# Low parts of the projection weights: kept in HBM by the first unit of tokens and read back by the second, in place of a second subtraction

## The chip, the cores and the metric

The kernel runs on one core of a Trainium2 chip. The metric is the device time of one execution in microseconds (us), the median of the runs shown. A core has a matrix engine (TensorE, PE in the profile; PEld is its weight load), three engines for elementwise work (VectorE or DVE, ScalarE or ACT, GpSimd or POOL), and SyncE (SP), which here issues every DMA, one after the other in the order in which they were emitted. An instruction that has to wait holds up what stands behind it on its engine.

## What is computed

The reference is a trunk of two layers over 2048 tokens of 1024 channels, all in float32. Cut to what matters:

```python
for i in range(2):
    h = rmsnorm(x, norm_g[i]) * (1.0 + scale) + shift        # scale, shift, gate from c
    out = rglru_block(h, ...) if i == 0 else gated_deltanet_block(h, ...)
    x = x + gate * out
return rmsnorm(x, final_g)

# both blocks begin with a projection:  proj = h @ in_w
#   layer 0: in_w is 1024 x 2048, then a causal convolution over 4 tokens, gates, a linear recurrence
#   layer 1: in_w is 1024 x 4096 (q, k, v, z) and 16 columns more, then the convolution and a
#            recurrence over chunks with a 128 x 128 state for each of 8 heads
```

## The kernel before, in words

**Splitting into high and low parts.** A float32 product is made of three matmuls on a faster, shorter type (float32r): each operand is split into a high part (the value rounded to that type) and a low part (the value minus its high part), and high times high, high times low and low times high are added up in PSUM; low times low is left out. `products` (line 646) emits these three matmuls for each of the 8 blocks of 128 input channels, 24 matmuls of 128 x 512 for one panel and one half of the tokens.

**Panels and units.** The weights of a projection are cut into panels of 128 output channels, 128 partitions x 1024 values, 512 KB. The tokens are cut into two units of 1024, and each unit into two halves of 512. The order of the whole program is: projection of layer 0 for unit 0 (`in1, 0`: 16 panels, called x and z) and for unit 1 (`in1, 1`), its output projection, projection of layer 1 for unit 0 (`in2, 0`: 32 panels, called k, v, q and z) and for unit 1 (`in2, 1`), and the last output projection. So each of the 48 panels is used twice, once in each unit, far apart in time.

**Getting a panel ready.** `panels_thread` (line 614) does this for every panel of every unit: SP loads it into a buffer `raw` (line 610), ACT rounds it into `whi` (line 639), and POOL subtracts, `wlo = raw - whi` (line 642). `raw`, `whi` and `wlo` have two buffers each. A new panel is begun when the panel two before it has made its last product; the third panel and the first and last two of a unit are loaded somewhat ahead. A panel makes two jobs of 24 matmuls, one for each half of the tokens.

**The other work of the stages.** In layer 0 each product of an x panel goes through ACT (copy to `xe`), POOL (first tap of the convolution, line 727), three more taps on DVE (line 701), then a split of its own (ACT `xh`, line 751; DVE `xl`, line 754) before the matmuls of the gates (`pg`, line 760). Besides, DVE sums rows of the conditioning weights (`acc`, line 415), which end in small matmuls (`adapt`, line 283). In layer 1 the same taps (line 701) make k, v and q; DVE inverts triangular blocks (`ttmp`, `tblk`, lines 1228 and 1231; a chain of small operations that each wait for the one before), and the recurrence passes between PE (`pp`, `py`, `pS`), DVE (`zt`, line 1357; `state`, line 1390) and ACT. Blocks are turned by way of HBM: `blk_d`, `tt_d`, `ac`, `v_d`, `q_d` are small transfers out and back on SP's queue.

**What sets the order.** The program is emitted by a planner (`Weave`, line 66). Every piece of work is a thread that yields the engine and an estimated duration before each step; the planner emits the step with the earliest estimated start. So the order on every engine is fixed when the program is built, from the estimates (2.3 us for the subtraction of a panel on POOL, for example). On the chip each engine runs its list in order and waits where data or a buffer is not there yet. The estimates know nothing of one engine slowing another.

Of the kernel before, what the change touches and what calls it, by code (L numbers as in the profile page):

```python
# [16 lines left out]
P = 128  # L17
# [24 lines left out]
class Slots:  # L42
    """The buffers of a tag, taken in turn."""
# [5 lines left out]
class Hold:  # L49
    """A buffer with several last readers."""  # L50
# [15 lines left out]
class Weave:  # L66
    """Emits threads of instructions in the order of their estimated start.

    Before each step a thread yields the engine, its duration and optionally the latency
    until the next step may start; for a transfer "sp", its bytes and whether to wait for  # L70
    its end. It yields an Event to wait for it, and Slots to take a buffer of them.
    """
# [66 lines left out]
def trunk_kernel(ctx, tc, x, c, ada_w, ada_b, ada_c, norm_c, final_g, w1, cw1, cb1, gate_w, gate_b, lam, ow1,  # L139
# [18 lines left out]
    def f(ap):  # L158
        return ap.bitcast(F32)
# [4 lines left out]
    # constants  # L164
# [37 lines left out]
    # tags: pool and number of buffers  # L202
# [11 lines left out]
    # free after the queries, before the recurrence ends  # L214
# [36 lines left out]
    def softplus(out, src, e, d):  # L251
        # max(x, 0) + log1p(exp(-|x|)), log1p(e) = 2 atanh(e / (2 + e))
        m = out
        dve.tensor_scalar(m, src, 0.0, None, ALU.min)
        dve.scalar_tensor_tensor(m, m, 2.0, src, ALU.mult, ALU.subtract)
        act.activation(e, m, AF.Exp)
        dve.tensor_scalar(d, e, 2.0, None, ALU.add)
        dve.reciprocal(out=d, in_=d)
        dve.tensor_tensor(e, e, d, ALU.mult)
        dve.tensor_tensor(d, e, e, ALU.mult)  # L260
        dve.tensor_scalar(m, d, 2.0 / 17.0, 2.0 / 15.0, ALU.mult, ALU.add)
        for q in (13, 11, 9, 7, 5, 3, 1):
            dve.tensor_tensor(m, m, d, ALU.mult)
            dve.tensor_scalar(m, m, 2.0 / q, None, ALU.add)
        dve.tensor_tensor(m, m, e, ALU.mult)
        dve.scalar_tensor_tensor(out, src, 0.0, m, ALU.max, ALU.add)

# [1 line left out]
    def finish_columns(layer, part, d, src):  # L269
        # bias, and for the scale (1 + scale) * norm_g  # L270
# [9 lines left out]
    def columns_of(acc, pt):  # L280
        # sums over the partitions, four columns of 128 channels
        for q in range(4):
            pe.matmul(pt[:, q:q + 1], lhsT=acc[:, q * P:(q + 1) * P], rhs=ones[:, 0:1], start=True, stop=True)
# [3 lines left out]
    def first_loads_thread():  # L287
        # scale and shift of the first layer, in the order in which they are needed
# [35 lines left out]
    def first_pe_thread():  # L324
        # scale, by the tensor engine
# [22 lines left out]
    def first_dve_thread():  # L348
        # shift, by DVE and the ones
# [47 lines left out]
    def row_halves_thread(parts):  # L397
        # halves of the other conditioning rows, summed over the channels of c by DVE and the ones
# [73 lines left out]
    def norm_thread(key, layer, src, t0, slot, before, after, xtags=("b4",) * TB, htag="hf"):  # L472
        # before: what the loads wait for; after: what the writes wait for
# [46 lines left out]
    def turned_thread(key, layer, src, t0, slot, before, between, after):  # L520
        # the norm of a tile, transposed ahead by 32 x 32 blocks, the blocks by way of memory
# [32 lines left out]
    def later(gen):  # L554
        # after the last transfer issued
        yield "none", w.free["dma"] + w.SEEN - w.now
        yield from gen
# [26 lines left out]
    # the panels of each unit in order, and its products: panel, half of the tokens  # L584
# [29 lines left out]
    def panels_thread():  # L614
        yield ev("adaissue", 2)
        ahead = []
        for name, panels, _ in plans:
            for m, p in enumerate(panels):
                # the third waits for the pair before it and is loaded ahead
# [15 lines left out]
                raw, rtok = ahead.pop(0)  # L635
                yield ev("raw", name, p)
# [3 lines left out]
                yield "pool", 2.3  # L640
                lo = tile_([P, KT, P], "wlo", "wlo", F32R)
                pool.tensor_tensor(lo, raw, f(hi), ALU.subtract)  # L642
                put("raw", rtok)
                w.set(ev("w", name, p), (hi, lo, htok, ltok))

    def products(pt, lhs, rhs, wait=None, dur=MM):
        # (hi + lo) * (hi + lo) without lo * lo
# [33 lines left out]
    def project_thread():  # L681
        for name, panels, jobs in plans:
# [3 lines left out]
            for n in range(len(jobs)):  # L686
                if name == ("in1", 0) and n < 2:
                    # the first two side by side, as the channels arrive
# [14 lines left out]
    def extend(xe, pt, mtok, carry, key, g):  # L703
        # the last columns of the half before, and the product
# [220 lines left out]
    def phase1_end_thread():  # L925
        # the memory of the first layer goes to the second
# [118 lines left out]
    def key_thread(u, h, i):  # L1045
        beta, gs, eg = yield ev("dec", u)
        # decay factors between the tokens of a chunk
# [19 lines left out]
        # row norms of k  # L1067
# [34 lines left out]
        # products of the keys  # L1102
# [22 lines left out]
        # k decayed to the end of the chunk  # L1125
# [30 lines left out]
    def tokens_of(ap, name):  # L1156
        # to token layout: transposed by 32 x 32 blocks, the blocks by way of memory
# [12 lines left out]
    def value_thread(u, h, i):  # L1170
        # v over the norm of k
# [33 lines left out]
    def inverses_thread(u, h):  # L1205
        # inverses of the 32 x 32 unit triangles on the diagonal
# [36 lines left out]
    def levels_thread(u, h):  # L1243
        # the transposed inverse takes the place of the transposed triangle, block by block
# [78 lines left out]
    def recurrence_thread(u, h):  # L1323
# [4 lines left out]
        for i in range(NTC):  # L1328
# [7 lines left out]
            for b in range(TB):  # L1336
                m = i * TB + b
                # no state before the first chunk, none needed after the last
# [21 lines left out]
                # a bank of PSUM is read by one engine at a time  # L1360
# [56 lines left out]
    def outputs_thread(u, h, i, oo, otok, so, sotok):  # L1417
# [14 lines left out]
        # transposed by 32 x 32 blocks: channel (e, i) of token (g, j) goes to partition (g, i)  # L1432
# [65 lines left out]
    def gated_thread(b, on, tok, zs, ztok):  # L1498
# [3 lines left out]
        # the blocks of the first units before the phase begins, in the place of panels  # L1502
# [26 lines left out]
    def out2_jobs():  # L1529
        nb = S // P  # L1530
        # the last columns in smaller parts
# [190 lines left out]
```

## Time and profile before

| | |
|---|---|
| time, median of 3 runs | 2044.7 us (2042.34 to 2049.82) |
| span of the profiled execution | 2033.7 us, 11.0 us under that median |
| busy in it | PE 1881.4 us (93%), DVE 1578.4 (78%), ACT 1019.8 (50%), POOL 945.0 (46%) |
| moved by DMA | 263.99 MB; read from HBM 186.38 MB, written 75.50 MB |
| subtraction of a panel on POOL | 96 times, 243.5 us in all |

The profile is of one execution. Its rows are read as follows. A group's row gives line, engine, operation, what it writes and reads, shape and count, then busy time and mean duration in ns, then how long the engine had been idle before these instructions and what ended that. A timeline row gives start, duration, engine, line, and in square brackets the engine's idle time before it and who ended it. A row of stretches gives the length, then busy time (and instructions) of PE, PEld, DVE, ACT and POOL, the granted clock of PE (1.00 is full speed), the busy share of the DMA engines and GB/s. The stages, as the panels' matmuls show them, are about: `in1, 0` from the start to 286 us, `in1, 1` to 536, the output projection to 725, `in2, 0` to 1276, `in2, 1` to 1838, and the last output projection.

### The profile page before, as it was taken

The page shows a single profiled execution, that of the slowest core. Times are in us where ns is not written, and L with a number is a line of the kernel's source. Part 1 is how long each engine was busy: PE and PEld are TensorE (multiplying, and loading weights), DVE is VectorE, ACT ScalarE, POOL GpSimd, SP SyncE. Part 2 cuts the span into 40 slices and gives each one's busy share as a digit, 9 for nine tenths or more (in the row PEclk, how much of TensorE's full clock was granted, in tenths as well). Part 3 has the DMA queues.
Part 4 walks back from the last instruction along what each step waited for, and adds up shares of the span by engine and source line. Part 5 has one row for each costly group of instructions (what it writes and reads, how often), then busy time and mean ns, then how long its engine had stood idle before and what let it go on. Part 6 is the DMA issues. An engine that isn't in the chain of part 4 may idle for free.

```text
span 2033.7 us, 31640 instructions
## 1 busy us (share of the span) xinstructions
PE 1881.4 (93%) x10408; PEld 1526.0 (75%) x10408; DVE 1578.4 (78%) x3176; ACT 1019.8 (50%) x2449; POOL 945.0 (46%) x1487
## 2 busy tenths in 40 slices
PE   6989889888999999999999999998999999999998
PEld 3777667676787777777787787777878777778887
DVE  6788998987744556988887988778888879887654
ACT  3656566454611224456565555554655555655311
POOL 4565665645400137545454653474455546531101
PEclk9999989989999999999999999999999999999999
DMA  8254524333368813436663436343334333466761
GB/s 315 60 150 128 186 98 134 122 109 119 125 195 215 252 54 96 102 70 148 143 144 82 89 86 173 84 113 93 69 91 104 90 79 83 111 184 210 227 197 63
DMA packets 493132, 263.99 MB, mean 130 GB/s; under 512 B 369188, under 2 KB 437028, under 8 KB 492968
## 3 DMA queue, kind: packets, MB, share of 16 engines
q1 hardware_dynamic: 492968, 261.97, 46.7%
q8 instruction: 82, 1.34, 0.3%
q14 instruction: 82, 0.67, 0.1%
HBM read 186.38 MB, written 75.50 MB: 129 GB/s over the span
## 4 chain that ended last, share of the span: by engine, by line
PE 39%; DVE 27%; DMA 8%; POOL 7%; issue 7%; ACT 6%; SPq 3%; DVEq 0%; POOLq 0%; ACTq 0%
PE mm L653 16%; PE mmo L653 12%; DVE xf L701 7%; DVE tblk L1231 3%; DVE ttmp L1228 3%; PE pg L760 2%; DMA raw<-in_w 2%; POOL wlo L642 1%; DVE ec L1100 1%; DMA xt_d<-xb 1%; SPq L515 1%; DVE acc L415 1%; POOL tz L798 1%; POOL xf L727 1%; DMA xt<-x_d 1%
## 5 line engine op out<-in xcount | busy, mean ns | idle before, releaser
L701 DVE SCALAR_TENSOR_TENSOR xf<-xe,cw_s,xf 128x512 f32<-128x512 f32 x384 | 359.8, 940 | 47.7 <-POOL xf L727 24.6
L642 POOL TENSOR_TENSOR wlo<-raw,whi 128x1024 fp32r<-128x1024 f32 x96 | 243.5, 2537 | 134.9 <-ACT whi L639 119.1
L1231 DVE TENSOR_TENSOR tblk<-tblk,ttmp 128x60 f32<-128x60 f32 (+24 forms) x496 | 144.3, 291 | 10.9 <-POOL tblk L1222 0.5
L1228 DVE TENSOR_TENSOR ttmp<-blk,tblk 128x60 f32<-128x60 f32 (+24 forms) x496 | 123.0, 248 | 16.9 <-DMA blk<-blk_d 6.5
L639 ACT CAST whi<-raw 128x1024 fp32r<-128x1024 f32 x96 | 100.2, 1044 | 47.3 <-DMA raw<-in_w 42.9
L716 POOL COPY carry<-xe 128x4 f32<-128x4 f32 x128 | 41.3, 322 | 170.6 <-ACT xe L713 158.8
L713 ACT COPY xe<-mm 128x512 f32<-128x512 f32 x128 | 74.1, 579 | 83.8 <-PE mm L653 79.8
L653 PE MATMUL mmo<-oh,yh 128*128 128x512 f32 x256 | 100.9, 394 | 5.1 <-DVE xr L908 4.7
L653 PE MATMUL mm<-hl_('in2', 1)_12407,whi 128*128 128x512 f32 x256 | 104.8, 410 | 0.0
L653 PE MATMUL mm<-hh_('in2', 0)_5394,whi 128*128 128x512 f32 x256 | 104.7, 409 | 0.0
L653 PE MATMUL mm<-hh_('in2', 0)_5171,whi 128*128 128x512 f32 x256 | 104.3, 407 | 0.3 <-ACT xe L713 0.3
L653 PE MATMUL mm<-hl_('in2', 0)_5395,whi 128*128 128x512 f32 x256 | 104.2, 407 | 0.0
L653 PE MATMUL mm<-hl_('in2', 1)_12235,whi 128*128 128x512 f32 x256 | 104.2, 407 | 0.0
L653 PE MATMUL mm<-hh_('in2', 0)_5394,wlo 128*128 128x512 f32 x256 | 104.1, 407 | 0.0
L653 PE MATMUL mm<-hh_('in2', 1)_12406,whi 128*128 128x512 f32 x256 | 104.0, 406 | 0.0
L653 PE MATMUL mm<-hl_('in2', 0)_5172,whi 128*128 128x512 f32 x256 | 103.8, 406 | 0.0
L653 PE MATMUL mm<-hh_('in2', 0)_5171,wlo 128*128 128x512 f32 x256 | 103.8, 405 | 0.0
L653 PE MATMUL mm<-hh_('in2', 1)_12234,whi 128*128 128x512 f32 x256 | 103.4, 404 | 0.2 <-DVE tz L972 0.2
L653 PE MATMUL mm<-hh_('in2', 1)_12406,wlo 128*128 128x512 f32 x256 | 103.6, 405 | 0.0
L653 PE MATMUL mm<-hh_('in2', 1)_12234,wlo 128*128 128x512 f32 x256 | 103.5, 404 | 0.0
L653 PE MATMUL mmo<-ol,oh 128*128 128x512 f32 (+1 forms) x264 | 102.1, 387 | 0.0
L653 PE MATMUL mmo<-oh,yl 128*128 128x512 f32 x256 | 100.8, 394 | 1.4 <-DVE yl L882 1.4
(326 smaller groups left out, 5910.8 us busy)
## 6 DMA issues: line engine op xcount, KB each, us to landing
raw<-in_w SPq DMA_DIRECT2D x96, 512.0 KB, 4.0
araw<-in_ada_w SPq DMA_DIRECT2D x32, 512.0 KB, 3.7
xt<-x_d SPq DMA_DIRECT2D x32, 512.0 KB, 4.5
xt_d<-xb SPq DMA_DIRECT2D x192, 64.0 KB, 2.4
xk<-xt_d SPq DMA_DIRECT2D x24, 512.0 KB, 4.7
xt<-in_x SPq DMA_DIRECT2D x16, 512.0 KB, 5.3
ada<-in_ada_w SPq DMA_DIRECT2D x16, 512.0 KB, 8.9
y_d<-tz SPq DMA_DIRECT2D x32, 256.0 KB, 2.7
```

The costliest lines, as they stand in the source:

```text
L415: dve.scalar_tensor_tensor(acc, raw[:, k, :], ck, acc, ALU.mult, ALU.add)
L515: sp.dma_start(out=dst[c_], in_=tb[32 * c_:32 * c_ + 32])
L639: act.copy(hi, raw)
L642: pool.tensor_tensor(lo, raw, f(hi), ALU.subtract)
L653: pe.matmul(pt, lhsT=lhs[a][:, k, :], rhs=rhs[b][:, k, :], start=(k == 0 and n == 0), stop=(k == KT - 1 and n == 2))
L701: dve.scalar_tensor_tensor(xf, xe[:, 1 + j:1 + j + TC], wc[:, j:j + 1], xf, ALU.mult, ALU.add)
L713: act.copy(xe[:, 4:4 + TC], pt)
L716: pool.tensor_copy(out=carry, in_=xe[:, TC:TC + 4])
L727: pool.tensor_scalar(xf, xe[:, 1:1 + TC], cw1_s[:, n, 0:1], cb1_s[:, n:n + 1], ALU.mult, ALU.add)
L760: pe.matmul(pg, lhsT=a[:, g, :], rhs=b, start=(q == 0), stop=(q == 2))
L1228: dve.tensor_tensor(tmp, blk[:, j, j + 1:32].unsqueeze(2).to_broadcast([P, r, c_]), t[:, j, 0:c_].unsqueeze(1).to_broadcast([P, r, c_]), A ...
L1231: dve.tensor_tensor(t[:, j + 1:32, 0:c_], t[:, j + 1:32, 0:c_], tmp, ALU.subtract)
```

## The change

In the first unit of tokens the low part is still made by the subtraction; after it, SP writes it to an HBM buffer of its own, one for each of the 48 panels (`keep_thread`). In the second unit there is no subtraction: SP reads that buffer into `wlo`, and the load of `raw` and the rounding into `whi` stay. The buffer `raw` is given back after the rounding in the second unit. In numbers of instructions: 48 subtractions of 128 x 1024 on POOL fewer, 48 DMA writes and 48 DMA reads of 512 KB more, all on SP's queue. The values of the low parts are the same. The diff, without lines of comment:

```diff
                 raw, rtok = ahead.pop(0)
+                lo = tile_([P, KT, P], "wlo", "wlo", F32R)
+                if name[1] > 0:
+                    kept = yield ev("kept", p)
+                    yield "sp", 512 * KB, False
+                    sp.dma_start(out=f(lo), in_=kept)
+                    w.spawn(arrive_thread(ev("lo", name, p)), 0)
                 yield ev("raw", name, p)
                 yield "act", 0.95
                 hi = tile_([P, KT, P], "whi", "whi", F32R)
                 act.copy(hi, raw)
-                yield "pool", 2.3
-                lo = tile_([P, KT, P], "wlo", "wlo", F32R)
-                pool.tensor_tensor(lo, raw, f(hi), ALU.subtract)
-                put("raw", rtok)
+                if name[1] > 0:
+                    put("raw", rtok)
+                    yield ev("lo", name, p)
+                else:
+                    yield "pool", 2.3
+                    pool.tensor_tensor(lo, raw, f(hi), ALU.subtract)
+                    put("raw", rtok)
+                    w.spawn(keep_thread(p, lo), 5)
                 w.set(ev("w", name, p), (hi, lo, htok, ltok))
 
+    def keep_thread(p, lo):
+        kept = dram.tile([P, KT, P], F32, name=f"wlo_d{p[0]}{p[1]}{p[2]}")
+        yield "sp", 512 * KB
+        sp.dma_start(out=kept, in_=f(lo))
+        w.set(ev("kept", p), kept)
```

Since the planner counts with other steps now, the order moves a little on every engine. Three places matter for what follows; in all rows a number behind `x` is how many such instructions stand in a row, and line numbers from 639 of the old file on stand 7 to 17 higher in the new one.

POOL in `in1, 1`, from the split of the gate weights (`gl`) of the last but one block of channels to that of the last, before:

```order
L828 TENSOR_TENSOR gl<-gw,gh 128x256
L798 TENSOR_TENSOR tz<-tz,tg 128x512
L716 COPY carry_109<-xe_3817 128x4
L727 TENSOR_SCALAR xf_3842<-xe_3817,cw_s,cb_s 128x512
L642 TENSOR_TENSOR wlo<-raw_3819,whi 128x1024
L778 TENSOR_SCALAR th<-th 128x512
L642 TENSOR_TENSOR wlo<-raw_3901,whi 128x1024
L828 TENSOR_TENSOR gl<-gw,gh 128x256
```

and the same stretch with the change:

```order
L845 TENSOR_TENSOR gl<-gw,gh 128x256
L815 TENSOR_TENSOR tz<-tz,tg 128x512
L728 COPY xe_3858<-carry_109 128x4
L733 COPY carry_109<-xe_3858 128x4
L744 TENSOR_SCALAR xf_3873<-xe_3858,cw_s,cb_s 128x512
L795 TENSOR_SCALAR th<-th 128x512 x2
L811 COPY hcar<-tg 128x1
L815 TENSOR_TENSOR tz<-tz,tg 128x512
L728 COPY xe_4025<-carry_109 128x4
L733 COPY carry_109<-xe_4025 128x4
L744 TENSOR_SCALAR xf_4044<-xe_4025,cw_s,cb_s 128x512
L845 TENSOR_TENSOR gl<-gw,gh 128x256
```

The two subtractions are gone, and the steps of the next block (`xe`, `carry`, `xf`) have moved up into their place.

SP in `in2, 1`, around the load of the panel q of head 4 (`tt_d` and `ac` are the way out and back of the inverted blocks, `blk_d` the way out of the next ones), before:

```order
L1239 DMA tt_d<-ttmp 256x1x32 x4
L1252 DMA ac<-tt_d 32x4x32 x3
L610 DMA raw_16082<-in_w 128x1024
L1252 DMA ac<-tt_d 32x4x32 x5
L1444 DMA o_d<-ob 32x16x32 x4
L1122 DMA blk_d<-ac 32x4x32 x3
```

and with the change:

```order
L1256 DMA tt_d<-ttmp 256x1x32 x4
L1461 DMA o_d<-ob 32x16x32 x3
L1269 DMA ac<-tt_d 32x4x32 x6
L610 DMA raw_16192<-in_w 128x1024
L641 DMA wlo<-wlo_d2q_9069 128x1024
L1269 DMA ac<-tt_d 32x4x32 x2
L1461 DMA o_d<-ob 32x16x32
L1139 DMA blk_d<-ac 32x4x32 x4
```

The read of the low part stands right behind the load of `raw`, and the last two `ac` and all of `blk_d` stand behind it.

SP in `in1, 0`, around the loads of the third and the fourth panel (`raw`), before:

```order
L820 DMA gw<-in_gate_w 128x256
L610 DMA raw_399<-in_w 128x1024
L530 DMA xt<-in_x 128x1024 x2
L610 DMA raw_674<-in_w 128x1024
L515 DMA xt_d<-xb 32x16x32 x8
```

and with the change:

```order
L837 DMA gw<-in_gate_w 128x256
L660 DMA wlo_d1x_356<-wlo 128x1024
L610 DMA raw_402<-in_w 128x1024
L660 DMA wlo_d1z_386<-wlo 128x1024
L530 DMA xt<-in_x 128x1024 x2
L660 DMA wlo_d1x_646<-wlo 128x1024
L610 DMA raw_680<-in_w 128x1024
L515 DMA xt_d<-xb 32x16x32 x8
```

The writes of the low parts of the first three panels stand between the loads now; the one of the third stands ahead of the second load.

## The prediction

> **What bounds the kernel now.** I read the page first, then the busy time by stage, then who PE waits for in the second unit's stages, then the rows around those waits. The page:
>
> ```profile
> span 2033.7 us, 31640 instructions
> PE 1881.4 (93%) x10408; PEld 1526.0 (75%) x10408; DVE 1578.4 (78%) x3176; ACT 1019.8 (50%) x2449; POOL 945.0 (46%) x1487
> ```
>
> PE is busy for 93% of the span, so nothing that leaves its work alone can gain more than its idle time and what it loses at a low clock. The change takes work from POOL, the least busy engine, so at first sight it frees what nobody waits for. The two stages in which it does so, as rows of stretches (`in1, 1`, then `in2, 1`):
>
> ```profile
> 286.00:536.00 250.00, 222.86 (x902) 177.84 (x901) 206.75 (x224) 144.30 (x190) 147.32 (x124) 0.92 0.36 117
> 1276.00:1838.00 562.00, 529.62 (x3493) 437.34 (x3493) 463.30 (x1191) 309.64 (x940) 294.35 (x550) 0.99 0.41 101
> ```
>
> PE is idle for 250.0 - 222.9 = 27.1 us in the first and 562.0 - 529.6 = 32.4 us in the second, and its granted clock is 0.92 in the first. DVE is busy for 83% and 82% of them. Whom PE waits for (total, times, longest), first `in1, 1`, then `in2, 1`:
>
> ```profile
> PE pg L760 <- DVE xl L754: 15.3, 5, 4.0
> PE adapt L283 <- DVE acc L415: 9.6, 3, 4.1
> ...
> PE pp L1348 <- DVE state L1390: 11.3, 8, 2.4
> PE py L1365 <- DVE zt L1357: 6.1, 5, 1.6
> PE pk L1073 <- DVE tblk L1231: 4.4, 1, 4.4
> PE pk L1073 <- DVE kt L961: 2.4, 2, 1.5
> PE pqk L1193 <- DVE qt L961: 2.3, 2, 1.3
> ```
>
> It is DVE: 24.9 of the 27.1 us and 26.5 of the 32.4 us. No row of PE's waits of any size names the subtraction; a panel is ready in time. So the path is PE, and where PE stands still, DVE.
>
> **Why DVE is late.** The same operation takes very different times (minimum, median, maximum in ns):
>
> ```profile
> L701 DVE SCALAR_TENSOR_TENSOR xf<-xe,cw_s,xf x384: 700/749/2921, 59.1 to 1795.2; 128x512 f32<-128x512 f32 x192
> L1112 DVE TENSOR_TENSOR ac<-pkk,ec x32: 649/691/693, 779.9 to 1788.7; 128x512 f32<-128x512 f32 x32
> ```
>
> One wait of PE in `in1, 1` with what stands around it:
>
> ```profile
> 467.86 2.34 POOL L642 TENSOR_TENSOR wlo<-raw,whi 128x1024 fp32r<-128x1024 f32 x1 [0.45 <-ACT whi L639]
> 467.87 2.88 DVE L701 SCALAR_TENSOR_TENSOR xf<-xe,cw_s,xf 128x512 f32<-128x512 f32 x1
> 470.68 0.68 DVE L754 TENSOR_TENSOR xl<-xf,xh 128x512 fp32r<-128x512 f32 x1
> 471.28 0.74 DVE L701 SCALAR_TENSOR_TENSOR xf<-xe,cw_s,xf 128x512 f32<-128x512 f32 x1
> 471.41 0.53 PE L760 MATMUL pg<-xl,gh 128*128 128x512 f32 x1 [4.02 <-DVE xl L754]
> ```
>
> And one of `in2, 1`, where the chain of small operations stands in front of the state:
>
> ```profile
> 1496.33 0.22 DVE L1231 TENSOR_TENSOR tblk<-tblk,ttmp 128x60 f32<-128x60 f32 x1
> 1496.43 2.40 POOL L642 TENSOR_TENSOR wlo<-raw,whi 128x1024 fp32r<-128x1024 f32 x1 [4.26 <-ACT whi L639]
> 1496.59 2.33 DVE L1228 TENSOR_TENSOR ttmp<-blk,tblk 128x66 f32<-128x66 f32 x1
> 1500.50 0.49 PE L1348 MATMUL pp<-state,kt 128*128 128x128 f32 x2 [1.54 <-DVE state L1390]
> ```
>
> The tap that starts 0.01 us after the subtraction takes 2.88 us, until the subtraction is over, and the next one 0.74; the step of the small chain takes 2.33 in place of 0.22. So a DVE operation that meets a panel's subtraction loses 2.88 - 0.74 = 2.1 us, and all that stands behind it on DVE comes as much later. The operations of line 1112, one of whose inputs is in PSUM, never take more than 0.693 us, so not every DVE operation is held up. How much of POOL's other work does the same, the rows leave open: POOL is busy for 147.3 of the 250 us of `in1, 1`, and yet the median of line 701, 749 ns, is close to its minimum.
>
> **The change part by part.** *48 subtractions less on POOL.* By their own length (2.34 and 2.40 us above) they cost PE nothing. They count by what they do to DVE. In `in1, 1` six of the eight waits in the two rows of 15.3 and 9.6 us have a panel's subtraction in them or just ahead; each loses the 2.1 us that DVE loses: 6 x 2.1 = 12.6 us. Bounds: 0, if DVE has other work in the place of the loss, and 24.9, if both rows go.
>
> *The clock.* Six stretches begin where those six waits end, and in them PE has half its clock (0.50):
>
> ```profile
> 294.30:301.00 6.70, 6.08 (x18) 4.71 (x19) 5.38 (x6) 3.32 (x5) 3.46 (x5) 0.50 0.47 169
> 328.40:335.20 6.80, 6.17 (x15) 4.82 (x16) 5.99 (x9) 5.16 (x7) 2.73 (x4) 0.50 0.76 251
> 410.30:417.10 6.80, 6.80 (x21) 5.64 (x22) 3.31 (x7) 2.94 (x5) 0.99 (x1) 0.50 0.23 79
> 441.10:444.40 3.30, 3.03 (x7) 2.45 (x8) 2.83 (x5) 1.09 (x3) 0.00 (x0) 0.50 0.24 88
> 471.80:475.10 3.30, 3.30 (x9) 2.58 (x8) 3.27 (x6) 2.19 (x4) 0.00 (x0) 0.50 0.00 0
> 502.50:505.80 3.30, 2.89 (x7) 2.31 (x8) 2.94 (x5) 0.69 (x1) 0.00 (x0) 0.50 0.64 185
> ```
>
> PE works 6.08 + 6.17 + 6.80 + 3.03 + 3.30 + 2.89 = 28.3 us in them at half speed and loses half of it, 14.1 us. The longest of the six waits, 4.02 us, would shrink by 2.1 to 1.9, while the one ahead of the third stretch was this long:
>
> ```profile
> 410.17 1.09 PE L283 MATMUL adapt<-ones,acc 128*128 128x1 f32 x5 [2.21 <-DVE acc L415]
> ```
>
> So 2.21 us was enough here for a fall and 1.9 may be: I count three quarters of 14.1, 10.6 us (bounds 0 and 14.1). The Trainium skill (TensorE: Matmul & The Clock Gate, Part 1) lets the clock fall after an idle window of about 3.4 us. By it no wait of 1.9 us could bring a fall and all 14.1 would be gained, a total of 2010; the wait of 2.21 us disagrees with it, and I go by the row.
>
> *`in2, 1`.* The five rows above make 26.5 us. A subtraction comes once for each of 32 panels, so one in about 562 / 32 = 17.6 us, and DVE has a queue behind it most of the time; but part of these waits is the recurrence's own latency, which stays. I take half, 13.2 us, for lack of a row that parts the two (bounds 0 and 26.5).
>
> *96 DMAs more.* They are 48 x 2 x 0.524 MB = 50 MB on top of 264. What such a transfer costs, and what it costs the one right behind it:
>
> ```profile
> q1 hardware_dynamic: 492968, 261.97, 46.7%
> raw<-in_w SPq DMA_DIRECT2D x96, 512.0 KB, 4.0
> on<-o_d SPq DMA_DIRECT2D x16, 512.0 KB, 5.1
> zs<-z_d SPq DMA_DIRECT2D x16, 512.0 KB, 6.5
> ```
>
> By the share, 50 MB more make the queues busy for 46.7% x 50 / 262 = 9% more of the span, about 56%, so they don't become the bound. `zs` is issued right behind `on` and lands 1.4 us later after its issue, so a small transfer that meets a read or a write is later by about that. A panel gets ready no later: the read, right behind `raw`, lands some 4.0 + 1.4 = 5.4 us after the issue, the chain that it replaces took 4.0 for `raw`, 1.04 for the rounding (80.65 below) and 2.4 for the subtraction. Its two buffers are what the reads wait for: the read of a panel may not start before PE is through with the panel two before, and SP, which issues in order, stands still until then, with `ac`, `blk_d` and `v_d` behind it. In the trace the widest lead of SP over PE of this kind:
>
> ```profile
> 1364.73 0.33 SPq L610 DMA_DIRECT2D raw<-in_w  x1
> 1385.51 0.39 PE L653 MATMUL mm<-hh_('in2', 1)_12406,wlo 128*128 128x512 f32 x1
> 1388.87 2.52 SPq L1239 DMA_DIRECT2D tt_d<-ttmp  x4
> ```
>
> SP would stand for 21.2 us, to 1385.9, but its next transfer was not ready before 1388.87 anyway. In the first unit the write waits for POOL's subtraction; the one that is moved past most is the write of the third panel, ahead of the load of the fourth:
>
> ```profile
> 43.74 0.33 SPq L610 DMA_DIRECT2D raw<-in_w  x1
> 73.63 2.40 POOL L642 TENSOR_TENSOR wlo<-raw,whi 128x1024 fp32r<-128x1024 f32 x1 [1.59 <-ACT whi L639]
> 80.65 1.04 ACT L639 CAST whi<-raw 128x1024 fp32r<-128x1024 f32 x1
> ```
>
> That load goes from 43.7 to about 76.4 and lands 4.0 us later, at 80.4, where its rounding began at 80.65: covered by a hair. For all of this I charge 5 us (an estimate: a few transfers late by 1.4 us where PE waits for what comes of them); bounds 0, and 56 as worked out below.
>
> **The sum.** -12.6 - 10.6 - 13.2 + 5 = -31.4 us on a span of 2033.7, so 2002.3; the median of the runs stood 11.0 over that span, and stays so: 2013.3 us. About 0.5%, 10 us, is what a measurement of this kernel can tell from no change.
>
> **The rivals.** *The waits stay.* DVE has a queue behind most waits, POOL's other operations hold it up too, and the planner, which counts 2.3 us less on POOL, asks for DVE's results earlier. Then half of the first two terms is left and nothing of the third: -6.3 - 5.3 + 5 = -6.6, so 2038, no change that can be told. For it: even with 2.1 us less for each panel DVE stays busy for about 70% of both stages, (206.8 - 16 x 2.1) / 250 and (463.3 - 32 x 2.1) / 562. Against it: the rows show the loss right in front of the waits, and the low median of line 701 beside a POOL that is busy for over half of the stage. The Trainium skill has a rule for this rival (SBUF — State Buffer, "Who interferes with whom"): a DVE instruction with two inputs in SBUF and any GpSimd instruction that reads SBUF shut each other out, the second one for as long as the first lasts. By it the other operations of POOL would hold DVE up as the subtraction does, and a total near this rival's 2038 would follow; the trace agrees for the subtraction (2.88 us) and speaks against it for most of the rest (749 ns).
>
> *SP behind PE: slower.* Each of the 48 reads holds up SP's queue until PE frees the buffer. What ACT's rounding waited for bounds that:
>
> ```profile
> L639 ACT CAST whi<-raw 128x1024 fp32r<-128x1024 f32 x96 | 100.2, 1044 | 47.3 <-DMA raw<-in_w 42.9 <-PE mm L653 4.2
> ```
>
> It waits for PE for only 4.2 us in all and for the load for 42.9, so SP mostly leads PE by less than the 4.0 us of a landing. If SP stood still for 1.2 us a read with transfers ready behind, and all of it came through the small chain to the state and to PE, that is 48 x 1.2 = 56 us: 2013.3 + 56 = 2069. It outweighs the gain from 31.4 / 48 = 0.65 us a read on. Against it: the 21.2 us above that nobody would have noticed.
>
> *All of it.* If the waits for DVE go whole, 24.9 + 14.1 + 26.5 = 65.5 us: 1979.
>
> That the subtractions stay can be ruled out: the order of POOL's instructions has 48 of them in place of 96.
>
> **How the numbers follow.** Forecast 0.66 (1993 to 2034), the waits stay 0.15, slower 0.11, all of it 0.08. Faster by over 0.5% is the first and the last, 0.74; within 0.5% is 0.15; slower 0.11. The range of 1988 to 2040 holds the forecast, most of the waits that stay, and leaves out the slow case and most of the largest gain.
>
> **What would show it.** In the changed profile: the taps of line 701 with a maximum near 0.75 us in `in1, 1` and `in2, 1` but for POOL's other work; DVE's busy time down by up to 48 x 2.1 = 101 us; PE's clock in `in1, 1` near 0.97; the waits of `pg` for `xl` there well under 15.3 us; SP's waits for PE at the reads without a wait of PE behind them. I am wrong if PE's idle time in these stages stays while DVE's busy time falls, if `in1, 0` or `in2, 0`, where the subtractions stay, get longer by more than 5 us, or if PE waits for what `ac` or `blk_d` bring.

## The result, and the profile after

The changed kernel takes 1984.46 us (median of 4 runs, 1979.51 to 1989.06), the kernel before beside it 2043.52 (4 runs): a ratio of 0.9704, 95% interval 0.9671 to 0.9737. That is 59 us less, where 31 were forecast, and 29 us under the forecast of 2013.3. The direction and the mechanism were right, two terms of the sum were much too small (12.6 us where 20.6 came, 13.2 where 25.3 came), and one was missing.

The page of the changed kernel, busy time of each engine, and its DMA queue:

```profile
span 1987.3 us, 31679 instructions
PE 1869.0 (94%) x10408; PEld 1520.6 (77%) x10408; DVE 1500.0 (75%) x3176; ACT 1025.1 (52%) x2453; POOL 811.3 (41%) x1439
...
q1 hardware_dynamic: 506792, 312.31, 55.5%
```

DVE is busy for 78.4 us less than before (1578.4), though it executes the same 3176 instructions; PE for 12.4 less with the same 10408. The queues' share of 55.5% is the 56% that was forecast. The stages as rows of stretches, in the order `in1, 0`, `in1, 1`, first output projection, `in2, 0`, `in2, 1`, last output projection:

```profile
0.00:292.00 292.00, 245.46 (x974) 187.40 (x975) 234.42 (x312) 163.37 (x235) 164.00 (x174) 0.93 0.59 190
292.00:508.00 216.00, 209.16 (x905) 168.52 (x904) 178.31 (x222) 147.50 (x192) 98.02 (x108) 0.98 0.52 169
508.00:701.00 193.00, 182.95 (x774) 147.01 (x773) 102.69 (x138) 48.10 (x60) 23.21 (x30) 0.97 0.71 205
701.00:1261.00 560.00, 519.11 (x3289) 423.85 (x3288) 456.91 (x1170) 297.75 (x895) 291.89 (x555) 0.99 0.53 135
1261.00:1793.00 532.00, 525.05 (x3526) 437.42 (x3525) 414.71 (x1188) 310.26 (x940) 211.10 (x517) 1.00 0.53 139
1793.00:1987.00 194.00, 187.22 (x949) 156.41 (x947) 113.00 (x150) 58.08 (x135) 23.07 (x58) 0.99 0.56 174
```

In `in1, 1` PE is now idle for 6.8 us in place of 27.1 and has a clock of 0.98 in place of 0.92; in `in2, 1` it is idle for 7.0 us in place of 32.4. A stage is measured from the last panel matmul of the stage before it to its own last one; the first output projection ends where the panel matmuls of `in2, 0` begin, and the last one with the span. The stages changed like this (us):

| stage | before | after | difference |
|---|---|---|---|
| `in1, 0` | 286.4 | 292.4 | +6.0 |
| `in1, 1` | 249.8 | 215.3 | -34.5 |
| first output projection | 188.9 | 193.4 | +4.5 |
| `in2, 0` | 551.1 | 560.3 | +9.2 |
| `in2, 1` | 561.7 | 531.4 | -30.3 |
| last output projection | 195.8 | 194.6 | -1.2 |

So 64.8 us were gained where the subtraction went, and 18.5 given back in stages that keep theirs or never had one. Whom PE still waits for, first in `in1, 1`, then in `in2, 1`:

```profile
PE adapt L283 <- DVE acc L415: 3.5, 3, 1.7
PE mm L670 <- ACT whi L646: 2.3, 1, 2.3
PE pg L777 <- DVE xl L771: 0.8, 3, 0.3
...
PE pS L1394 <- ACT yt L1388: 4.0, 6, 1.6
PE pd L1079 <- POOL el L1075: 1.3, 4, 0.5
PE pp L1365 <- DVE state L1407: 1.0, 2, 0.7
PE pk L1090 <- DVE ttmp L1245: 0.2, 1, 0.2
```

The waits for DVE fell from 24.9 to 4.3 us and from 26.5 to 1.2. The taps of DVE (line 701 before, 718 now) in `in2, 0`, where POOL still subtracts, and in `in2, 1`, where it doesn't:

```profile
L718 DVE SCALAR_TENSOR_TENSOR xf<-xe,cw_s,xf x144: 702/746/2859, 708.2 to 1219.3; 128x512 f32<-128x512 f32 x144
...
L718 DVE SCALAR_TENSOR_TENSOR xf<-xe,cw_s,xf x144: 703/752/886, 1281.3 to 1746.5; 128x512 f32<-128x512 f32 x144
```

The long taps are gone with the subtraction; the median never moved. What SP and ACT wait for because of the reads:

```profile
SPq L641 <- PE mm L670: 93.1, 31, 18.2
...
L646 ACT CAST whi<-raw 128x1024 fp32r<-128x1024 f32 x96 | 100.3, 1045 | 52.8 <-DMA raw<-in_w 43.5 <-PE mm L670 9.0
```

SP does stand at 31 of the 48 reads, for 93.1 us in all, and behind that ACT's rounding waits only 5.5 us more than before (52.8 against 47.3). PE waits for one panel, 2.3 us.

### The profile page after: what moved, and what is told of

The parts are those of the page before. It is cut to its first block, busy times and chain, and to the rows that moved or that the text cites. A ratio compares the mean times of both kernels' runs of the same rounds, so it can differ in the third digit from the quotient of the medians.

```text
span 1987.3 us, 31679 instructions
## 1 busy us (share of the span) xinstructions
PE 1869.0 (94%) x10408; PEld 1520.6 (77%) x10408; DVE 1500.0 (75%) x3176; ACT 1025.1 (52%) x2453; POOL 811.3 (41%) x1439
## 3 DMA queue, kind: packets, MB, share of 16 engines
q1 hardware_dynamic: 506792, 312.31, 55.5%
## 4 chain that ended last, share of the span: by engine, by line
PE 50%; DVE 20%; DMA 10%; POOL 6%; issue 5%; ACT 5%; SPq 4%; DVEq 0%; POOLq 0%; ACTq 0%
PE mm L670 25%; PE mmo L670 12%; DVE xf L718 5%; DVE tblk L1248 2%; DVE ttmp L1245 2%; PE pg L777 2%; SPq L515 1%; DMA raw<-in_w 1%; DMA pq<-q_d 1%; DVE acc L415 1%; PE pp L1365 1%; PE py L1382 1%; DMA ada<-in_ada_w 1%; PE pS L1394 1%; PE pS L1395 1%
## 5 line engine op out<-in xcount | busy, mean ns | idle before, releaser
L718 DVE SCALAR_TENSOR_TENSOR xf<-xe,cw_s,xf 128x512 f32<-128x512 f32 x384 | 327.8, 855 | 54.9 <-POOL xf L961 32.0
L652 POOL TENSOR_TENSOR wlo<-raw,whi 128x1024 fp32r<-128x1024 f32 x48 | 122.3, 2548 | 81.0 <-ACT whi L646 67.9
L646 ACT CAST whi<-raw 128x1024 fp32r<-128x1024 f32 x96 | 100.3, 1045 | 52.8 <-DMA raw<-in_w 43.5
L670 PE MATMUL mm<-hh_('in2', 0)_5430,wlo 128*128 128x512 f32 x256 | 105.1, 411 | 0.0
L670 PE MATMUL mm<-hl_('in2', 0)_5431,whi 128*128 128x512 f32 x256 | 105.1, 410 | 0.0
L670 PE MATMUL mm<-hl_('in2', 1)_12333,whi 128*128 128x512 f32 x256 | 104.8, 409 | 0.0
L670 PE MATMUL mm<-hh_('in2', 0)_5430,whi 128*128 128x512 f32 x256 | 104.4, 408 | 0.0
L670 PE MATMUL mm<-hh_('in2', 1)_12332,wlo 128*128 128x512 f32 x256 | 104.3, 408 | 0.0
L670 PE MATMUL mm<-hh_('in2', 1)_12512,wlo 128*128 128x512 f32 x256 | 104.1, 407 | 0.0
L670 PE MATMUL mm<-hl_('in2', 0)_5208,whi 128*128 128x512 f32 x256 | 103.6, 405 | 0.0
L670 PE MATMUL mm<-hh_('in2', 0)_5207,wlo 128*128 128x512 f32 x256 | 103.5, 404 | 0.0
L670 PE MATMUL mm<-hh_('in2', 1)_12512,whi 128*128 128x512 f32 x256 | 103.5, 404 | 0.0
```

Of the source, the lines that this page charges most:

```text
L646: act.copy(hi, raw)
L670: pe.matmul(pt, lhsT=lhs[a][:, k, :], rhs=rhs[b][:, k, :], start=(k == 0 and n == 0), stop=(k == KT - 1 and n == 2))
L718: dve.scalar_tensor_tensor(xf, xe[:, 1 + j:1 + j + TC], wc[:, j:j + 1], xf, ALU.mult, ALU.add)
```

## The experiments

Theory: a subtraction on POOL shuts out DVE's operations with two inputs in SBUF, what stands behind on DVE comes late, and PE waits for it and loses its clock. Rival A: the planner's new order helps (or `raw`, which comes free sooner). Rival B: POOL's own other work no longer stands behind the subtraction. All ratios are to the kernel before, run on the same chip beside each kernel (its medians lay between 2043.4 and 2045.0 us).

| run | what is different | us | ratio, 95% interval |
|---|---|---|---|
| e1 | changed kernel + the subtraction, uncounted | 2066.6 | 1.0106, 1.0079 to 1.0133 |
| e2 | changed kernel + one-input work on POOL, uncounted | 2031.4 | 0.9939, 0.9923 to 0.9956 |
| e3 | change in the first layer alone | 2018.5 | 0.9873, 0.9850 to 0.9896 |
| e4 | change in the second layer alone | 2014.7 | 0.9858, 0.9838 to 0.9878 |
| e7 | changed kernel, 2.3 us on POOL counted, nothing there | 2000.5 | 0.9796, 0.9764 to 0.9828 |
| e5 | as e7, the subtraction there | 2071.6 | 1.0140, 1.0103 to 1.0178 |
| e6 | as e7, wide one-input work there | 2028.9 | 0.9936, 0.9913 to 0.9960 |
| e9 | as e7, small powers there | 2011.9 | 0.9837, 0.9818 to 0.9856 |
| e8 | before, second unit's subtraction on DVE | 1997.9 | 0.9788, 0.9749 to 0.9828 |
| e10 | changed kernel, no write and no read | 1981.8 | 0.9690, 0.9670 to 0.9710 |
| e11 | before, all subtractions on DVE | 1957.1 | 0.9569, 0.9539 to 0.9598 |
| e12 | changed kernel, first unit's subtraction on DVE | 1969.8 | 0.9630, 0.9613 to 0.9648 |
| e13 | changed kernel, writes not counted | 1990.2 | 0.9722, 0.9691 to 0.9753 |
| e14 | before, DVE's loss counted | 2034.2 | 0.9952, 0.9933 to 0.9971 |

### The subtraction put back, and other work in its place (e1, e2)

```diff
                     put("raw", rtok)
-                    yield ev("lo", name, p)
+                    yield ev("lo", name, p); pool.tensor_tensor(raw, raw, f(hi), ALU.subtract)
```

> The changed kernel, and in the second unit POOL also makes the 48 subtractions again, into raw, where nobody reads them. The planner isn't told, so every engine's list is that of the changed kernel, with 48 instructions more on POOL's. Theory (POOL's subtraction shuts out DVE's operations with two inputs in SBUF, and PE waits for what DVE brings late): the waits of PE for DVE come back to some 20 us each in in1, 1 and in2, 1, the clock of in1, 1 falls to 0.92 or 0.93, and the time is 2030 to 2050 us. Rival A (what helps is the planner's new order, or the buffer raw that comes free sooner): 1980 to 1995 us, as the changed kernel. Rival B (what helps is that POOL's own other work isn't queued behind the subtraction): 2030 to 2050 here as well, so the next run has to part it from the theory.

In e2 this stands there instead:

```diff
+[pool.tensor_scalar(r, r, 0.5, 0.5, ALU.mult, ALU.add) for r in (raw, raw[:, 0:5, :])]
```

> As the run before, but in place of each of the 48 subtractions POOL makes two operations with one input (TENSOR_SCALAR in place on raw, 128x1024 and 128x640, some 1.5 + 0.9 us by the 757 ns of a 128x512 one). POOL is as busy as with the subtraction, DVE's two-input operations lose at most a little (under such POOL operations 3 of 39 of DVE's were slow before). Theory (the lock by the two-input operation): 1980 to 1997 us, PE waits for DVE under 8 us in each of in1, 1 and in2, 1, taps of DVE stay near 0.75 us. Rival B (POOL's queue): 2025 to 2050 us. If any POOL operation that reads SBUF shuts DVE out, as the Trainium skill states (SBUF — State Buffer, Who interferes with whom): as the run before, 2030 to 2050, with taps up to 2.9 us.

e1 took 2066.6 us, 82 more than the changed kernel and more than the theory's 2050. So rival A falls as the whole of the gain. e2 was meant to part the theory from rival B and did not. It came out at 2031.4, on rival B's side; but its operations held DVE up too (taps up to 1.6 us in `in2, 1`; the 3 slow of 39 that its expectation leant on are 15 of 39 in e6's), and POOL stood at a place that nobody had planned:

```profile
L718 DVE SCALAR_TENSOR_TENSOR xf<-xe,cw_s,xf x144: 702/751/1605, 1299.5 to 1788.1; 128x512 f32<-128x512 f32 x144
...
PE pd L1079 <- POOL eh L1075: 4.5, 5, 1.0
...
PE pd L1079 <- POOL el L1075: 3.8, 7, 0.8
```

In e2 PE waits for POOL (`eh`, `el`) for 8.3 us in `in2, 1` where it is 1.3 in the changed kernel. So both the place on POOL and the form of the operation had to be held fixed.

### The same place, four contents (e7, e5, e6, e9)

```diff
-                    put("raw", rtok)
+                    yield "pool", 2.3; ...; put("raw", rtok)
```

Where the dots are stands nothing (e7), `pool.tensor_tensor(raw, raw, f(hi), ALU.subtract)` (e5), `pool.tensor_scalar(r, r, cw2_s[:, 0, 0:1], 0.0, ALU.mult, ALU.add)` on 1024 and on 640 columns of `raw` (e6), or twice `pool.tensor_tensor(raw[:, 0, 0:4], ones[:, 0:4], mhalf[:, 0:4], ALU.pow)` (e9). The planner sees the same in all four, so the lists of PE, DVE, ACT and SP are the same, row by row.

> The changed kernel, but the planner goes on counting 2.3 us on POOL for each of the 48 panels, for which nothing is emitted: the order is planned as if the subtraction were there, and raw is given back after it. Theory (lock): 1980 to 1998 us, since nothing shuts DVE out. Rival A (the gain is the planner's new order, or raw coming free sooner): 2015 to 2045 us.

> The same lists on every engine as in the run with 2.3 us counted and nothing emitted, and the subtraction stands on POOL's list where it was counted (into raw, read by nobody). The place is planned now, where the first such run put it wherever the low part had arrived. Theory (lock): 2035 to 2060 us, as before plus what the writes and reads cost, PE waiting for DVE some 20 us in each of in1, 1 and in2, 1. Rival A: no more than 10 us over the run with nothing emitted.

> Again the same lists; in place of the subtraction POOL makes two TENSOR_SCALAR whose factor comes from SBUF, as in the first tap of the convolution (line 961), under which 4 of 24 of DVE's operations were slow, where under the form with two constants 15 of 39 were (line 795). 128x1024 and 128x640, some 2.4 us in all. Theory (lock, and POOL's time by itself costs little): 1980 to 2003 us, DVE's excess under these operations below 5 us. Rival B (POOL's queue): within 15 us of the run with the subtraction. Between the two, say 2015, both would have a part.

> Once more the lists of the run with 2.3 us counted and nothing emitted. POOL's place is taken by two small powers of 128x4 (line 249's operation, some 1.1 us each), under which none of 20 of DVE's taps was slow: POOL is busy as long as with the subtraction and holds nobody up by it. Theory (DVE shut out): 1995 to 2008 us, as the 2000.5 with nothing emitted. Rival B (POOL's own work comes late behind it): 2015 to 2030 us, since the scaled copies that took about as long gave 2028.9.

The same three taps of DVE in `in2, 1`, and the matmul `py` that waits for what follows on DVE, first in e5:

```profile
1679.20 4.24 DVE L718 SCALAR_TENSOR_TENSOR xf<-xe,cw_s,xf 128x512 f32<-128x512 f32 x3
1679.87 2.37 POOL L648 TENSOR_TENSOR raw<-raw,whi 128x1024 f32<-128x1024 f32 x1 [2.31 <-ACT whi L646]
...
1685.07 0.34 DVE L1374 SCALAR_TENSOR_TENSOR zt<-pp,eg,vn 128x128 f32<-128x128 f32 x1
1685.46 0.49 PE L1382 MATMUL py<-zt,ac 128*128 128x128 f32 x2 [0.92 <-DVE zt L1374]
```

and in e9, where POOL is as long at its two small powers:

```profile
1633.97 2.08 DVE L718 SCALAR_TENSOR_TENSOR xf<-xe,cw_s,xf 128x512 f32<-128x512 f32 x3
1634.64 2.27 POOL L648 TENSOR_TENSOR raw<-ones,mhalf 128x4 f32<-128x4 f32 x2 [2.32 <-ACT whi L646]
1638.23 0.35 DVE L1374 SCALAR_TENSOR_TENSOR zt<-pp,eg,vn 128x128 f32<-128x128 f32 x1 [0.48 <-PE pp L1366]
1639.19 0.38 PE L1382 MATMUL py<-zt,ac 128*128 128x128 f32 x2
```

The three taps take 4.24 us under the subtraction and 2.08 beside the powers: 2.16 us lost. `py` starts 6.26 us after the first tap in the one and 5.22 in the other. In e5 `zt` starts with no idle time of DVE before it, so DVE's queue is late, and PE waits 0.92 us; in e9 DVE has caught up and waits for PE. `in2, 1` of e5, e9 and e7 as rows of stretches:

```profile
1289.00:1860.00 571.00, 534.90 (x3495) 441.97 (x3494) 458.81 (x1185) 309.59 (x940) 291.07 (x549) 0.98 0.49 127
```

```profile
1268.00:1802.00 534.00, 522.07 (x3493) 435.06 (x3492) 408.40 (x1181) 309.70 (x940) 273.86 (x580) 1.00 0.52 136
```

```profile
1263.00:1796.00 533.00, 521.33 (x3493) 435.15 (x3493) 407.78 (x1184) 308.81 (x940) 211.01 (x515) 1.00 0.52 136
```

From e7 to e9 POOL gets 63 us of work more and the stage grows by one; from e9 to e5 POOL gets 17 more, DVE's busy time rises by 50 and the stage grows by 37. `in1, 1` takes 220.5 us in e7, 226.9 in e9 and 247.1 in e5. Over the whole kernel e5 is 60 us above e9: that is what the shutting out costs, with the time that POOL itself loses by it. e9 is 11 us above e7 (the intervals just overlap): rival B has a part, and a small one, most of it in `in1, 1`. All three runs missed what the theory gave: e9 lay 4 us over it, e5 12 and e6, for which it gave 1980 to 2003, 26. That e6 lies between, at 2028.9, fits its wide one-input operations, which hold DVE up as well, for less time each: of the 16 operations of DVE (taps and `xl`, lines 718 and 771) that began with more than 0.1 us of the 128x1024 form left, 11 were slow (by over 0.1 us) and 0.49 us was the mean loss of the 16, where under the subtractions of e5 15 of 16 were slow and 1.88 us was the mean.

e7 itself is 16 us above the changed kernel with nothing more to do, just over the theory's upper end: the same work in another order. 9 of the 16 lie in the last output projection, where the change touches nothing (203.9 us against 194.6).

### One layer alone (e3, e4)

```diff
-                if name[1] > 0:
+                if name[1] > 0 and p[0] == 1:
```

at the read and at the rounding, and at the write `if p[0] == 1` (2 in e4).

> The change for the 16 panels of the first layer alone; the second layer subtracts twice, as before. Theory: in1, 1 as in the changed kernel (some 215 us in place of 250), in2, 1 as before (some 562), and a part of the 18 us that in1, 0, the first output projection and in2, 0 got longer by: 2008 to 2022 us. By my forecast's terms this was to be 23 us less than before, or 2020. Rival A (a matter of the order as a whole): no sum of parts, anything from 1985 to 2045.

> The change for the 32 panels of the second layer alone. Theory: in2, 1 as in the changed kernel (some 532 us in place of 562), in1, 1 as before (some 250); in2, 0 keeps the 32 writes and, if these are what made it 9 us longer, stays at 560, else goes back to 551: 2010 to 2025 us, and with the run before the two gains make up 50 to 68 us. By my forecast's terms this was to be 13 us less than before, or 2031. Rival A: no sum of parts.

Both came out in the theory's range: 2018.5 and 2014.7, which is 26.6 and 30.3 us under the kernel before (2045.0) and together 57 of the change's 59. `in1, 1` takes 217.6 us in e3, `in2, 1` 531.5 in e4, and the other of the two is 3 to 4 us above that of before (565.7, 252.9). `in1, 0` is 293.4 in e3 and 285.1 in e4, so its 6 us come with the first layer's change. `in2, 0` is 556.2 in e3, without a write in it, and 559.9 in e4.

### What the transfers cost (e10, e13)

```diff
-                    sp.dma_start(out=f(lo), in_=kept)
...
-        sp.dma_start(out=kept, in_=f(lo))
```

> The changed kernel with the 48 writes and the 48 reads planned but not issued; in the second unit the high part is multiplied in the low part's place, so the low part's product is left out there. All else stands in the same order. It prices the transfers. Forecast's term: +5 us, so 1975 to 1985. Theory now (from +27.6 us between before and the run that subtracts in the planned place, and the 6 us that in1, 0 and the 9 us that in2, 0 grew by): the transfers cost 12 to 28 us, so 1956 to 1973.

In e13 the writes are there and not counted:

```diff
-        yield "sp", 512 * KB
+        yield "none", 0.0
```

> The changed kernel, but the planner doesn't count the 48 writes, so that up to the end of in1, 0 every engine but SP has its list of before, with the writes on SP's. If the 18 us by which in1, 0, the first output projection and in2, 0 grew come from the planner's other order: in1, 0 ends at 286 +- 3 (292 in the changed kernel, 291 with no transfer issued), and the time is 1965 to 1980 us. If they are scatter of an execution, or come from SP standing at the writes: in1, 0 ends at 290 to 295, 1980 to 1995 us.

Without any of the 96 transfers e10 takes 1981.8 us, 2.7 less than the changed kernel (the difference of the two ratios is 0.0014, with some 0.004 of uncertainty): the forecast's term of 5 us stands, and the theory that I had put against it falls. Its `in1, 0` still takes 291.3 us and its `in2, 0` 561.6, so these longer stages aren't the transfers' doing. In `in1, 0` the wait that grew is that of `pg` for `xl`. Before, then in the changed kernel, then in e10:

```profile
PE pg L760 <- DVE xl L754: 15.6, 11, 4.5
```

```profile
PE pg L777 <- DVE xl L771: 20.6, 9, 5.2
```

```profile
PE pg L777 <- DVE xl L771: 20.0, 9, 5.3
```

and in e13, which up to the end of that stage has the lists of before on all engines but SP:

```profile
PE pg L777 <- DVE xl L771: 14.4, 8, 4.5
```

Yet by its own expectation e13 doesn't decide: its 1990.2 us lie in the range of the second reading, and its 289.7 us for `in1, 0` between the two. For `in1, 0` the traces of all the runs do decide. Five kernels have the lists of before there, up to its last 10 us and on all engines but SP (before, e4, e8, e13, e14): the stage takes 285.1 to 289.7 us, the longest in e13, which has the writes. Nine have the lists of the changed kernel (that one, e1, e2, e3, e5, e6, e7, e9, e10): 291.3 to 295.5 us, the shortest in e10, which has none. So the 6 us are the planner's order, which moved when it began to count the writes. For `in2, 0` e10 shows that it isn't the transfers; e13 takes 563.2 us there, and what in the order makes this stage 9 us longer stays open.

### The subtraction on DVE (e8, e11, e12), and the loss counted (e14)

e8, and e11 without the conditions:

```diff
-                yield "pool", 2.3
+                yield ("dve", 1.4) if name[1] > 0 else ("pool", 2.3)
...
-                pool.tensor_tensor(lo, raw, f(hi), ALU.subtract)
+                (dve if name[1] > 0 else pool).tensor_tensor(lo, raw, f(hi), ALU.subtract)
```

> The kernel before, with the second unit's 48 subtractions on DVE, counted at 1.4 us, and nothing written to HBM or read back. POOL is as free as in the changed kernel, and nobody shuts DVE out, but DVE has 48 x 1.4 = 67 us more to do where the lock took 84. Theory (lock): what DVE gets back it spends, so 2020 to 2045 us. Rival B (POOL's queue): 1985 to 2005, since POOL's queue is as short as in the changed kernel.

> The kernel before, with all 96 subtractions on DVE (counted 1.4 us, measured 1.25) and no transfers added. Theory: the second unit gains as in the run that moved 48 of them (2044.0 to 1997.9), and the first, where DVE lost 83.6 us under 48 subtractions and would spend 60, gains some 20 to 45 more: 1950 to 1980 us. Rival (DVE is the bound in in1, 0, where it is busy for 82%): 1990 to 2010.

e12 makes the same exchange in the branch of the first unit of the changed kernel.

> The changed kernel, with the first unit's 48 subtractions on DVE. Theory: 1940 to 1970 us, 20 to 45 less than the changed kernel. Rival: no gain, 1980 to 1995, if what in1, 0 and in2, 0 wait for is DVE's own work.

e14 only counts, in the kernel before:

```diff
-                put("raw", rtok)
+                put("raw", rtok); w.free["dve"] = max(w.free["dve"], w.now - 2.5) + (1.75 if name[1] > 0 else 0)
```

> The kernel before, with POOL's subtraction in both units and nothing more emitted; in the second unit the planner counts 1.75 us on DVE for each panel when the subtraction runs. DVE loses as much as before, but the order knows of it. If what made 48 subtractions on DVE (counted) so much cheaper than the lock (not counted) is that the order knows: 2000 to 2030 us. If it is the loss itself, and where it falls can't be planned: 2035 to 2055 us.

On DVE a subtraction takes half of POOL's time; e8's row, then e11's:

```profile
L642 DVE TENSOR_TENSOR wlo<-raw,whi 128x1024 fp32r<-128x1024 f32 x48 | 59.8, 1247 | 8.5 <-ACT whi L639 8.3
```

```profile
L642 DVE TENSOR_TENSOR wlo<-raw,whi 128x1024 fp32r<-128x1024 f32 x96 | 119.5, 1245 | 22.2 <-ACT whi L639 22.2
```

e8 missed the theory's 2020 to 2045 by far: 1997.9, only 13 us over the changed kernel although DVE has 60 us more to do. That is in rival B's range, but e9 against e7 gives POOL's time only some 11 us. So 60 us of work that stand at a place of their own in DVE's list cost much less than the loss, which made DVE's busy time 78.4 us longer than in the changed kernel and strikes whatever stands there when the subtraction begins. That the planner knows of it is a part only: e14, where it knows of the loss and the loss stays, gains 9 us, between what either reading had given. The rest of the difference isn't shown. e12 met the time that was expected, but gained 15 us on the changed kernel where 20 to 45 were expected: its `in1, 0` and `in2, 0` are 20.8 and 34.9 us shorter than there, and its `in2, 1`, which has the same work, is 22.8 longer (554.2 against 531.4), for a reason that no run shows. e11 came out as expected and is the best version of all: 1957.1 us, 4.3% under the kernel before and 1.4% under the changed one (27 us), without a byte more of DMA.

## Why the prediction was wrong in its size

**What bounds the kernel.** Right: PE, and where it stands still DVE. **Why DVE is late.** Right: e5 against e9 shows it with every list but POOL's held fixed. The remark on line 1112 holds too. Over the trace of before, of DVE's operations that began with more than 0.1 us of a subtraction left, all 75 that read two inputs from SBUF were slow (by over 0.1 us), and none of the 14 two-input ones with an input in PSUM, and none of 23 transposes.

**The six waits of `in1, 1`, -12.6 us.** Too small: 24.9 - 4.3 = 20.6 us went. The step that failed is "each loses the 2.1 us that DVE loses". DVE's busy time in the stage fell by 206.75 - 178.31 = 28.4 us, and a loss stays in its queue until DVE next stands still. So a wait can collect the losses of several operations, and a subtraction that isn't next to a wait counts too. The five waits of `pg` for `xl` lost 15.3 - 0.8 = 14.5 us, 2.9 each. And one of the two waits that I had left out, since no subtraction stands next to it, shrank from 4.05 us to 0.78; before, then with the change:

```profile
359.03 2.69 POOL L642 TENSOR_TENSOR wlo<-raw,whi 128x1024 fp32r<-128x1024 f32 x1 [2.27 <-ACT whi L639]
359.38 4.07 DVE L415 SCALAR_TENSOR_TENSOR acc<-araw,c_col,acc 128x512 f32<-128x512 f32 x2
...
372.23 0.99 PE L283 MATMUL adapt<-ones,acc 128*128 128x1 f32 x6 [4.05 <-DVE acc L415]
```

```profile
366.27 0.94 PE L283 MATMUL adapt<-ones,acc 128*128 128x1 f32 x7 [0.78 <-DVE acc L415]
```

The subtraction hits the two sums at 359.38, and from there to 372.23 DVE never stands still (line 798's product on POOL, at 367.49, holds up one more sum on the way).

**The clock, -10.6.** Near, a little small: PE's busy time fell by 222.9 - 209.2 = 13.7 us, almost all of the bound of 14.1. The argument on where the clock falls was poor, though. It goes on falling after waits that are shorter than the 1.9 us of which I said that it may; the changed kernel in `in1, 1`, the wait and the stretch behind it, twice:

```profile
299.55 1.05 PE L283 MATMUL adapt<-ones,acc 128*128 128x1 f32 x8 [1.75 <-DVE acc L415]
...
392.34 1.02 PE L283 MATMUL adapt<-ones,acc 128*128 128x1 f32 x8 [0.93 <-DVE acc L415]
```

```profile
301.50:304.80 3.30, 3.30 (x9) 2.64 (x8) 2.68 (x4) 2.45 (x4) 1.62 (x3) 0.50 0.25 103
393.70:396.90 3.20, 3.20 (x9) 2.44 (x8) 1.33 (x3) 1.29 (x3) 0.00 (x0) 0.50 0.91 332
```

Both times eight one-column matmuls follow the wait. The Trainium skill (TensorE: Matmul & The Clock Gate, Part 1) has the clock fall after an idle window of some 3.4 us; these two rows disagree with it, as the 2.21 us of before did, even if the one-column matmuls are counted as idle (1.75 + 1.05 = 2.80 us and 0.93 + 1.02 = 1.95). What was gained came from fewer waits, not from their being under a limit.

**`in2, 1`, -13.2.** Half of what came: 26.5 - 1.2 = 25.3 us of waits, and 30.3 of the stage. The step "part of these waits is the recurrence's own latency, which stays" failed: e7, with nothing on POOL and another order, keeps 2.5 us of `py` for `zt` and nothing for `state`, and the changed kernel 1.0 us for `state` and nothing for `zt`. There was no row for the half, and the bound was right.

**96 DMAs, +5.** Right: 2.7 us, not to be told from nothing. SP's stands at the reads (93.1 us) were covered, as the 21.2 us had shown.

**What the sum left out.** The planner's other order as a whole. It was treated only where a queue is moved past; yet `in1, 0`, the first output projection and `in2, 0` grew by 19.7 us in the changed kernel and, but for the output projection, in e10 as well (that projection takes from 187.5 to 199.0 us in the traces of these kernels, so its 4.5 us may be scatter). That was named as a sign of being wrong ("get longer by more than 5 us"); it came true, in `in1, 0` by the order and in `in2, 0` not by the transfers, where the sum had a term for the transfers alone. In e5 the order, with the subtraction in its place, stands 28 us over the kernel before, so the change is, in medians, +28 for the order and the transfers, -60 for the lock, -11 for POOL's time, and -16 for the order once the 2.3 us aren't counted.

**From the span to the median, +11.0.** Failed as well: the changed kernel's median lies 2.8 us under its profiled span. The profiled execution of before lies at the low end (a span of 2033.7, where the runs have a median of 2043.5), that of the changed kernel at the high end (its own time is 1989.06, the longest of the four). Of the 29 us between forecast and result, 2002.3 - 1987.3 = 15.0 lie in the span and 11.0 + 2.8 = 13.8 here.

**The rivals.** "All of it", at 8%, had the mechanism right: 65.5 us foretold, 64.8 found in the two stages. "The waits stay" leant on the median of line 701, 749 ns beside a busy POOL. A median of 384 taps says nothing of the few that begin under a wide operation. Counted in the trace of before as above, for DVE's operations with two inputs in SBUF: under the subtraction 75 of 75 were slow; under POOL's other wide two-input operations (lines 798, 828 and 576, 128x256 and 128x512) 43 of 44; under its one-input operations of 128x512 (lines 778, 944 and 727) 66 of 97, by some 0.35 us; under its small powers (line 249, 128x1 and 128x4) none of 199. So the rule of the Trainium skill (SBUF — State Buffer, "Who interferes with whom") held for the wide two-input operations and in part for the wide one-input ones. It did not hold for the small ones: under e9's powers of 128x4, which read SBUF too, none of 119 was slow. "SP behind PE" didn't come: PE waited for one panel, 2.3 us. (Its price was added up wrongly: 48 x 1.2 is 57.6 us, so 2071.)

## What to carry to other kernels

The price of an operation on a little-used engine is what it does to the others: look at the longest executions of a common form on the neighbouring engine, see what they overlap, and charge all of the stage's waits behind that engine, not only those next to it. Where the order is planned from estimates, a run in which the estimate is kept and the work left out tells the order's share from the work's. If POOL's wide work holds up DVE, try DVE for the work itself as well: with all 96 subtractions there (e11) the kernel was 27 us below the way by HBM, with the second unit's alone (e8) 13 above it.

## What the runs showed of the hardware

In the trace of before 27 taps and `xl` of DVE began with more than 0.1 us of POOL's 128x1024 subtraction left. All of them ended 0.55 us after the subtraction did; they lost 1.99 us on the mean, with 2.19 us of the subtraction left when they started. POOL pays as well: of the 96 subtractions the 50 that started while DVE still had more than 0.1 us to go on an operation that reads SBUF alone (transposes left out) took 2.62 us in the median and up to 3.31, the other 46 took 2.39 and up to 2.41. Of POOL's operations, length in time alone doesn't decide: two powers of 128x4 take 2.27 us in e9 and hold nobody up. Whether it is their width or their kind, no run parts. And a stage that the change doesn't touch can differ by 9 us with the planner's order: the last output projection took 194.6 to 195.8 us in nine of these kernels and 201.4 to 203.9 in the other seven. From the changed kernel to e7 nearly the whole difference lies ahead of the last 646 matmuls, which are the same list in both and begin 45.9 and 54.9 us after `in2, 1` ends.
